# Hybrid decoder layer: other queue places for a SiLU, a reciprocal with its scaling, and the sums of the modulation

## The chip, the cores and the metric

The kernel runs on one core of a Trainium2 chip. The metric is the time of one execution on the device, in microseconds (us). The median of three executions before the change is 1846.04 us (1845.93 to 1848.33).

Five engines work side by side, each through a queue of its own: TensorE (PE in the profile, its weight loads PEld), VectorE (DVE), ScalarE (ACT), GpSimd (POOL) and SyncE (SP). In this kernel SP and POOL mostly issue DMA transfers. An instruction that waits holds up everything behind it in the same queue.

## The reference, cut to what matters

One layer of a hybrid decoder, 1024 tokens by 1024 channels, float32. Two branches start from the same projection: windowed attention with sinks, and a gated delta rule with 8 heads of 128 channels. Their gated sum passes an output projection and a norm, and an MLP of 4096 channels follows. A conditioning vector `c` gives six rows of modulation (`c_act @ w_ada + b_ada`). The change touches the delta rule's output and four of those rows:

```python
o = _gated_delta_rule(q, k, v, beta, g)                # head by head: a scan over chunks of tokens
o = o * lax.rsqrt(jnp.mean(jnp.square(o), -1, keepdims=True) + RMS_EPS) * norm_w
o = o * jax.nn.silu(z.reshape(shp))
...
mod = c_act @ w_ada[l] + b_ada[l]                      # shift, scale, gate rows
```

## The kernel before, in words

All large products are matmuls with a 512-column moving operand; float32 operands are split into a high and a low part, so that a product takes three matmuls. The kernel counts these large matmuls in `count[0]`, and this count is its clock for planning. `at(p, f)` puts the work `f` at count `p`, and `after(n, f)` n matmuls from now. Before each large matmul the events that are due are written out. So TensorE, VectorE and ScalarE have one fixed program order, written by hand; SP and POOL are ordered by the tile framework, by dependence.

The change lies in the stage of the heads. There, 24 projection units (`units_h`, 48 large matmuls each, through the line L261) fill TensorE: the q and v of each head and the gate `gb`. Between them the scan of the 8 heads runs, head `h` from count `R = R0 + 120 h`. Each head has 8 chunks of 128 tokens, one per 15 matmuls, in three steps 5 matmuls apart:

- `hd_a` at 0: TensorE multiplies the state (L1221), and VectorE makes `rhs` (L1223).
- `hd_b` at 5: TensorE multiplies `rhs` by the solved triangle (L1231), and ScalarE scales the result to `vn` (L1233).
- `hd_c` at 10: TensorE uses `vn` for the next state (L1242, added up by VectorE in L1247 and L1250) and for the output (L1254, L1255). ScalarE squares the output for the norm (L1257), VectorE copies it to `o` (L1258).

So each chunk goes through ScalarE once while TensorE does five large matmuls, and L1242 stands behind `vn` in TensorE's order.

Around the scan, the work of the other heads is placed: convolutions of q and v (ScalarE L1011 and L1012, VectorE taps L1016, ScalarE SiLU L1026), transposes and squares of q (L1166, L1170), products of k and q (L1182), transposes of v with ScalarE copies (L1205, L1209), the triangle of the next head (`hd_x`, L1147, with `hd_z` of the head after it, L1137), and the split of the next weights (ScalarE L232, VectorE L236).

For three kinds of work a small planner chooses the count. `vec(lag, cost, f)` and `act(lag, cost, f)` ask `window` for the first place from now + lag on. Per cycle of 15 matmuls VectorE has two windows (2 to 11 and 12 to 16.5) and ScalarE has one (7 to 19.5, so into the next cycle). A request uses up 0.68 of its cost in matmuls; if it doesn't fit any more, it moves to the next window. `now` writes work at a given count and books its cost. Outside the heads' range (`R0` to `R0 + 960`) `window` returns the count that was asked for.

The four parts that the change touches:

- **z.** `hd_gate` (at R + 35) loads the head's z into the tile `sz`, which exists once; POOL issues the load (L1121). The tile comes free when the previous head's result, which is written into the same tile (`hd_out`, L1287, at R + 45 and R + 60 of this head), has been stored (L1290). `hd_silu` applies SiLU to both halves on ScalarE (L1125).
- **The norm.** `hd_norm` (2 matmuls after the last chunk, so at 2 of the next head) adds two vectors on VectorE (L1263, L1264) and asks for `root`. `root` takes the square root on ScalarE (L1273), then come the reciprocal on VectorE (L1274), and the scaling of `o`, the even chunks on VectorE (L1270), the odd ones on ScalarE (L1268).
- **The output.** `hd_out` transposes `o` (L1284) and multiplies it with SiLU(z) (L1287).
- **The modulation.** Every 13 matmuls `ada_load` sends 256 KB of `w_ada` through SP (L1050) into one of three buffers, and VectorE adds it up (`ada_add`, L1058 and L1060). After eight of them `ada_part` sums over the partitions on TensorE (L1069).

When the last head is done (R0 + 960), the last `gb` unit runs, interleaved over its halves, and then the first unit of the next stage, the product with `w_oa`. In between ScalarE and VectorE split the attention's output into `ah` and `al` (`attn_split`, L218 and L219), and ScalarE empties the two PSUM banks of the `gb` unit (L1298). A unit takes two banks of the three of its kind.

Of the kernel before, what the change touches and what calls it, by code (L numbers as in the profile page):

```python
# [21 lines left out]
NT = S // P  # L22
# [12 lines left out]
def hybrid_layer_kernel(ctx: ExitStack, tc: tile.TileContext,  # L35
                        x, c, w_ada, b_ada, w_in, conv_w, a_log, dt_bias, sinks, dn_norm_w,
                        w_oa, w_ob, w_out, ln1_g, ln1_b, w_ff1, b_ff1, w_ff2, b_ff2,
                        ln2_g, ln2_b, out, dbg=None):
    nc = tc.nc
    x, c, out = x[0], c[0], out[0]  # L40
# [6 lines left out]
    V, A, G, T = nc.vector, nc.scalar, nc.gpsimd, nc.tensor  # L47
# [152 lines left out]
    def at(p, f, *args):  # L200
        order[0] += 1
        heapq.heappush(events, (p, order[0], f, args))

    def after(n, f, *args):
        at(count[0] + n, f, *args)
# [113 lines left out]
    def ada_load(blk):  # L319
        for i in range(2):  # L320
            t = ada_tile([P, 2, 4, P])
            for sec in (0, 1):
                nc.sync.dma_start(out=t[:, sec, :, :], in_=w_ada2[:, sec, 4 * i:4 * i + 4, blk * P:(blk + 1) * P])
            adav.setdefault(blk, []).extend(t[:, :, k, :] for k in range(4))
# [43 lines left out]
    for step in 'a0 x a1 x d a2 x a3 x a4 x a5 x a6 x a7 x'.split():  # L368
        if step == "x":
            x_load()  # L370
        elif step == "d":
            dk_raw = [load_raw(*wseq.pop(0)) for _ in range(2)]
            wdk = [parts_of(*r) for r in dk_raw]
        else:
            ada_load(int(step[1:]))
# [84 lines left out]
    for step in steps.split():  # L460
        f, k = step[0], int(step[1])
# [49 lines left out]
    with tc.tile_pool(name="pa", bufs=2, side="right") as pa:  # L511
# [120 lines left out]
        for h in range(8):  # L632
# [7 lines left out]
            for half in range(2):  # L640
                tp = psum("c", 1) if half else psum("b", 2)
                for j in range(4):
                    n = 4 * half + j
                    T.transpose(tp[:, j * P:(j + 1) * P], kT[:, n * P:(n + 1) * P], ident)
                for j in range(4):
                    n = 4 * half + j
# [16 lines left out]
            for half in range(2):  # L663
                kk = psum("a", 2)
                for j in range(4):
                    n = 4 * half + j
                    kc = kT[:, n * P:(n + 1) * P]
                    T.matmul(kk[:, j * P:(j + 1) * P], lhsT=kc, rhs=kc, start=True, stop=True)
                for j in range(4):
                    n = 4 * half + j  # L670
# [291 lines left out]
    def window(kind, p, cost):  # L962
        if not R0 <= p < R0 + 8 * PER:
            return p
        c, cost = int(p - R0) // 15 - 1, 0.68 * cost
        while True:
            for i, (start, cap) in enumerate({"V": ((2, 9), (12, 4.5)), "A": ((7, 12.5),)}[kind]):
                w = R0 + 15 * c + start
                q = max(p, w + used.get((kind, c, i), 0))
                if q + min(cost, cap) <= w + cap:  # L970
                    used[kind, c, i] = q + cost - w
                    return q
            c += 1
# [3 lines left out]
    def vec(lag, cost, f, *args):  # L977
        q = window("V", count[0] + lag, cost)
        at(q, f, *args)
        return q  # L980
# [9 lines left out]
    def act(lag, cost, f, *args):  # L990
        q = window("A", count[0] + lag, cost)
        at(q, f, *args)
        return q

    flags, padded = set(), []
# [49 lines left out]
    def ada_cols_of(f):  # L1045
        return (2, 5, 3, 4)[f // 2] * D + (f % 2) * HALF

    def ada_load(i, f, k):
        w, lo = ada["w"][i % 3], ada_cols_of(f)
        nc.sync.dma_start(out=w, in_=w_ada[k * P:(k + 1) * P, lo:lo + HALF])  # L1050
        q = vec(28, 3.3, ada_add, w, k)
        if k == KT - 1:
            at(q + 7, ada_part, f)

# [30 lines left out]
    for i, (f, k) in enumerate(items):  # L1085
        at(Q0 + 170 + 13 * i, ada_load, i, f, k)
# [40 lines left out]
    def o_chunk(d, n):  # L1127
        return d["o"][n // 4][:, chunk(n % 4)]
# [131 lines left out]
    def hd_norm(h):  # L1260
        d = heads[h]
        fs = pc.tile([P, NT], F32, tag="fs", name="fs")
        V.tensor_scalar(out=fs, in0=d["ssq"], scalar1=RMS_EPS * P * P, scalar2=None, op0=ALU.mult)  # L1263
        V.tensor_tensor(out=fs, in0=fs, in1=d["sso"], op=ALU.add)  # L1264

        def sc(n):
            if n % 2:
                A.activation(out=o_chunk(d, n), in_=o_chunk(d, n), func=AF.Copy, scale=fs[:, n:n + 1])  # L1268
            else:
                V.tensor_scalar(out=o_chunk(d, n), in0=o_chunk(d, n), scalar1=fs[:, n:n + 1], scalar2=None,  # L1270
                                op0=ALU.mult)
        def root():
            A.activation(out=fs, in_=fs, func=AF.Sqrt, scale=1.0 / P, bias=eps_q)  # L1273
            after(4, lambda: V.reciprocal(out=fs, in_=fs))  # L1274
            vec(5, 5.5, lambda: [sc(n) for n in range(0, NT, 2)])
            act(5, 7, lambda: [sc(n) for n in range(1, NT, 2)] + [flags.add(("o", h))])
        act(3, 7, root)

    def hd_out(h, half):
# [22 lines left out]
    for h in range(8):  # L1302
        R = R0 + PER * h
        early = max(R - 118, OPEN + 1)
        at(early, hd_load, h)
        for half in range(2):
            at(R - 45 + 15 * half, hd_kq, h, half)
            at(R - 40 + 15 * half, hd_qturn, h, half)
            at(R - 10 + 15 * half, hd_vturn, h, half)
            at(R + 75 + 5 * half, hd_silu, h, half)  # L1310
        if h == 0:
            at(early + 50, hd_z, 0)
            at(early + 52, hd_solved, 1)
        at(R - 55 if h else R0 - 30, hd_x, h)
        at(R + 35, hd_gate, h)
        for n in range(NT):
            at(R + 3 * HOP * n, hd_a, h, n)
            at(R + 3 * HOP * n + HOP, hd_b, h, n)
            at(R + 3 * HOP * n + 2 * HOP, hd_c, h, n)
        at(R + PER + 2, hd_norm, h)  # L1320
        at(R + PER + 45, hd_out, h, 0)
        at(R + PER + 60, hd_out, h, 1)
# [304 lines left out]
    for s in range(4):  # L1627
        q, t0 = (0, 1, 1, 0)[s], 4 * (s // 2)
# [324 lines left out]
    for s in range(7 * NS):  # L1953
        p = G0 + 24 * s
        at((p15 + 16, p15 + 28, p15 + 62, p15 + 64)[s] if s < 4 else p - 96 - 28, s_load, s)
        for j in range(2):
            if s < 2:
                q = p15 + (52, 68)[s] + 8 * j
            elif s >= 6 * NS:
                q = p - (94 if s > 6 * NS else 70) + (6 if s == 7 * NS - 1 else 10) * j  # L1960
            else:
                q = p - 46 + 10 * j
# [18 lines left out]
    for i, m in seq:  # L1981
        w, k0, mv, ab, begin = PROD[m]
# [152 lines left out]
```

## Time and profile before

| | |
|---|---|
| median of three executions | 1846.04 us |
| profiled execution | 1845.55 us, span 1843.8 us |
| TensorE busy | 1806.9 us (98%), mean granted clock 0.991 |
| VectorE, ScalarE, GpSimd busy | 1256.9, 1021.6, 309.8 us |
| heads' stretch, 560 to 960 us | TensorE busy 379.83 of 400 us, clock 0.97 |
| stretch before it, 192 to 560 us | TensorE busy 367.35 of 368 us, clock 1.00 |

A busy engine is one that has an instruction under way; the granted clock says at which share of its speed TensorE ran meanwhile. So a loss of TensorE can show up twice: as idle time, and as busy time at a lower clock. In a timeline, each row has the start, the duration, the engine, the line of the code, the operation, the tiles (`out<-in`) with shapes, the number of instructions that were merged, and in square brackets the idle time of the engine before it and what ended it. In a table of waits, a row says who waited for whom, the total, the number of times and the longest.

### The profile page before, as it was taken

The numbers are of one execution on the slowest core, as the hardware profiler recorded it, in microseconds if no ns is written. First come the engines' busy times: TensorE is split into PE (matmuls) and PEld (weight loads), VectorE is DVE, ScalarE is ACT, GpSimd is POOL, SyncE is SP. The second block draws the span as 40 slices with busy tenths as digits, with TensorE's granted clock in tenths as the row PEclk, the third lists the DMA queues.
The fourth block names the chain that finished last, engine by engine and source line by source line (L and its number), as shares of the span: only waits on it lengthen the run. The fifth ranks groups of instructions, "written<-read, shape, count | busy, mean of one in ns | idle before, by whom it ended". The sixth has DMA issues, their size and how long they took to land.

```text
span 1843.8 us, 26325 instructions
## 1 busy us (share of the span) xinstructions
PE 1806.9 (98%) x9185; PEld 1517.6 (82%) x9185; DVE 1256.9 (68%) x2366; ACT 1021.6 (55%) x2320; POOL 309.8 (17%) x466
## 2 busy tenths in 40 slices
PE   8999999999999999999889999999999999999998
PEld 6988888888888887888778888888888888888887
DVE  7688588888845565667344345788777776576697
ACT  4699678888765554555354223456555555434441
POOL 0233234443340011100001000001122220000000
PEclk8999999999999999999999999999999999999999
DMA  9666722232264556565447444358888879855671
GB/s 280 199 204 200 223 76 90 72 99 72 81 246 136 169 157 168 162 184 167 146 157 245 152 145 160 115 171 282 293 296 282 269 271 391 280 187 178 194 267 46
DMA packets 265686, 346.12 MB, mean 188 GB/s; under 512 B 26593, under 2 KB 171698, under 8 KB 265298
## 3 DMA queue, kind: packets, MB, share of 16 engines
q1 hardware_dynamic: 225938, 220.27, 38.2%
q0 software_dynamic: 31472, 107.39, 17.2%
q10 hardware_dynamic: 8144, 16.78, 2.5%
q8 instruction: 72, 1.18, 0.3%
q14 instruction: 60, 0.49, 0.1%
HBM read 235.59 MB, written 106.70 MB: 186 GB/s over the span
## 4 chain that ended last, share of the span: by engine, by line
PE 46%; issue 3%; ACT 2%; DVE 1%; DMA 0%; ACTq 0%; POOL 0%; DVEq 0%; POOLq 0%
PE mm L261 10%; PE mm L1996 8%; PE mm L2056 7%; PE a L2056 4%; PE b L1996 4%; PE b L2056 4%; PE a L1996 3%; PE mm L1622 2%; PE c L2056 2%; PE a L1622 1%; PE c L1622 1%; PE c L1996 0%; ACT mh L218 0%; ACT wh L218 0%; DMA sz<-z_d 0%
## 5 line engine op out<-in xcount | busy, mean ns | idle before, releaser
L261 PE MATMUL mm<-uh,wh 128*128 128x512 f32 x800 | 321.7, 402 | 0.0
L261 PE MATMUL mm<-uh,wl 128*128 128x512 f32 x800 | 321.6, 402 | 0.0
L261 PE MATMUL mm<-ul,wh 128*128 128x512 f32 x800 | 320.1, 400 | 0.0
L219 DVE TENSOR_TENSOR sp<-sraw,sp 128x1024 fp32r<-128x1024 f32 x112 | 132.7, 1219 | 75.9 <-ACT sp L218 75.9
L218 ACT ACTIVATE sp<-sraw 128x1024 fp32r<-128x1024 f32 x112 | 112.6, 1053 | 121.4 <-PE b L2056 75.4
L261 PEld LDWEIGHTS mm<-uh,wh 128*128 128x128 f32 x800 | 151.9, 190 | 26.6
L261 PEld LDWEIGHTS mm<-uh,wl 128*128 128x128 f32 x800 | 151.9, 190 | 26.2
L261 PEld LDWEIGHTS mm<-ul,wh 128*128 128x128 f32 x800 | 151.6, 189 | 26.3
L2056 PE MATMUL mm<-sp 128*128 128x512 f32 x528 | 136.0, 390 | 0.0
L2056 PEld LDWEIGHTS mm<-sp 128*128 128x128 f32 x528 | 98.7, 188 | 20.5 <-DVE sp L219 0.3
L2056 PE MATMUL a<-sp 128*128 128x512 f32 x336 | 92.2, 389 | 0.0
L824 DVE CUSTOM_DVE_ANT_0 nscore<-a,amask,nsink 128x256 f32<-128x256 f32 (+1 forms) x128 | 54.5, 463 | 43.7 <-PE a L817 43.4
L236 DVE TENSOR_TENSOR wl<-wr,wh 128x1024 fp32r<-128x1024 f32 x66 | 81.1, 1229 | 2.3 <-ACT wh L232 2.2
L1233 ACT ACTIVATE vn<-a,brk 128x128 f32<-128x128 f32 x64 | 23.4, 366 | 103.3 <-PE a L1231 103.1
L2056 PE MATMUL b<-sp 128*128 128x512 f32 (+1 forms) x336 | 79.6, 374 | 0.0
L2056 PEld LDWEIGHTS a<-sp 128*128 128x128 f32 x336 | 63.1, 188 | 13.1
L2056 PEld LDWEIGHTS b<-sp 128*128 128x128 f32 x336 | 60.3, 188 | 11.2
L232 ACT ACTIVATE wh<-wr 128x1024 fp32r<-128x1024 f32 x66 | 69.4, 1051 | 0.1
L835 POOL TENSOR_TENSOR sm<-sm 128x256 f32<-128x256 f32 x56 | 51.5, 920 | 103.8 <-ACT sm L831 73.0
L219 DVE TENSOR_TENSOR wl<-fraw,wh 128x1024 fp32r<-128x1024 f32 x43 | 52.5, 1221 | 19.6 <-ACT wh L218 19.6
L831 ACT ACTIVATE sm<-nscore,stat 128x257 f32<-128x257 f32 (+1 forms) x128 | 62.0, 487 | 2.7 <-DVE stat L824 2.5
L218 ACT ACTIVATE wh<-fraw 128x1024 fp32r<-128x1024 f32 x43 | 45.0, 1055 | 31.0 <-PE b L1996 24.8
(542 smaller groups left out, 4693.6 us busy)
## 6 DMA issues: line engine op xcount, KB each, us to landing
wr<-in_w_in_dram SPq DMA_DIRECT2D x60, 512.0 KB, 3.7
sraw<-hf_d SPq DMA_DIRECT2D x54, 512.0 KB, 4.4
adaw<-in_w_ada_dram SPq DMA_DIRECT2D x74, 256.0 KB, 5.0
fraw<-in_w_ff_dram SPq DMA_DIRECT2D x32, 512.0 KB, 5.4
sraw<-wt_d SPq DMA_DIRECT2D x32, 512.0 KB, 4.4
hf_d<-t ACTq DMA_DIRECT2D x48, 256.0 KB, 4.5
wt_d<-wx POOLq DMA_DIRECT2D x48, 256.0 KB, 3.6
sraw<-in_w_ff_dram SPq DMA_DIRECT2D x22, 512.0 KB, 4.9
```

Source lines behind the costliest of these rows:

```text
L218: A.activation(out=hi, in_=src, func=AF.Copy)
L219: after(lag, lambda: V.tensor_tensor(out=lo, in0=src, in1=hi.bitcast(F32), op=ALU.subtract))
L232: A.activation(out=hl[0], in_=raw, func=AF.Copy)
L236: V.tensor_tensor(out=hl[1], in0=raw, in1=hl[0].bitcast(F32), op=ALU.subtract)
L261: T.matmul(ts[half], lhsT=w[:, k, :], rhs=xx[k][:, sl], start=k == 0 and m == 0, stop=k == KT - 1 and m == 2)
L824: V.tensor_tensor_reduce(out=ns[:, i, 1:1 + W], in0=sc[:, i * 2 * P:i * 2 * P + W], in1=amask[:, mo:mo + W], scale=-1.0, scalar=nsink[:, 2 ...
L831: A.activation(out=sm[:, i, 0:1 + W], in_=ns[:, i, 0:1 + W], func=AF.Exp, scale=-1.0, bias=st[:, i:i + 1], accum_out=st[:, 2 + i:3 + i])
L835: G.tensor_tensor(out=sm[:, :, 1 + P:1 + 2 * P], in0=sm[:, :, 1:1 + P], in1=sm[:, :, 1 + P:1 + 2 * P], op=ALU.add)
L1233: after(1, lambda: A.activation(out=vn, in_=Wp[:, 0:P], func=AF.Copy, scale=brk[:, n, h:h + 1]))
L1622: T.matmul(pt, lhsT=m[k][:, tok], rhs=w[:, k % 2, :], start=k == 0 and w is wh and m is mh, stop=k == KT - 1 and m is ml)
L1996: T.matmul(pt, lhsT=a[:, kk, :], rhs=b[k], start=begin and k == 0 and x_ == 0, stop=k == 3 and x_ == 2, skip_group_check=True)
L2056: T.matmul(to, lhsT=a[:, f, t * P:(t + 1) * P], rhs=b[:, f, lo:up], start=(begin or own) and s % NS == 0 and f == 0 and x_ == 0, stop=s % ...
```

## The change

Three edits, in the counts and helpers that place work; the instructions themselves stay the same.

1. `hd_silu` moves from R + 75 and R + 80 to R + 122 and R + 130, which is 2 and 10 matmuls into the next head's scan.
2. In `root`, the reciprocal goes from a fixed 4 matmuls later to VectorE's planner, 9 matmuls later, at a cost of 0.5; both halves of the scaling are asked for 11 instead of 5 matmuls later.
3. `ada_add` is asked for 33 instead of 28 matmuls after its load was written.

```diff
     def ada_load(i, f, k):
         w, lo = ada["w"][i % 3], ada_cols_of(f)
         nc.sync.dma_start(out=w, in_=w_ada[k * P:(k + 1) * P, lo:lo + HALF])
-        q = vec(28, 3.3, ada_add, w, k)
+        q = vec(33, 3.3, ada_add, w, k)
         if k == KT - 1:
             at(q + 7, ada_part, f)
...
             A.activation(out=fs, in_=fs, func=AF.Sqrt, scale=1.0 / P, bias=eps_q)
-            after(4, lambda: V.reciprocal(out=fs, in_=fs))
-            vec(5, 5.5, lambda: [sc(n) for n in range(0, NT, 2)])
-            act(5, 7, lambda: [sc(n) for n in range(1, NT, 2)] + [flags.add(("o", h))])
+            vec(9, 0.5, lambda: V.reciprocal(out=fs, in_=fs))
+            vec(11, 5.5, lambda: [sc(n) for n in range(0, NT, 2)])
+            act(11, 7, lambda: [sc(n) for n in range(1, NT, 2)] + [flags.add(("o", h))])
...
             at(R - 10 + 15 * half, hd_vturn, h, half)
-            at(R + 75 + 5 * half, hd_silu, h, half)
+            at(R + 122 + 8 * half, hd_silu, h, half)
```

## The prediction

> **What bounds the kernel now.** I read the page first, then busy time by stretch, then the waits of the heads' stretch, and then the timeline around the longest of them.
>
> ```profile
> span 1843.8 us, 26325 instructions
> ...
> PE 1806.9 (98%) x9185; PEld 1517.6 (82%) x9185; DVE 1256.9 (68%) x2366; ACT 1021.6 (55%) x2320; POOL 309.8 (17%) x466
> ```
>
> ```profile
> 192.00:560.00 368.00, 367.35 (x1936) 314.41 (x1935) 283.39 (x688) 278.65 (x848) 145.83 (x185) 1.00 0.38 121
> 560.00:960.00 400.00, 379.83 (x2302) 324.57 (x2301) 236.06 (x549) 210.86 (x619) 32.29 (x53) 0.97 0.53 156
> ```
>
> TensorE is busy for 98% of the span, so only its gaps and its clock leave something to gain. The second view (length, busy time of PE, PEld, DVE, ACT and POOL, granted clock, DMA share) puts both losses into the heads' stretch: 400 − 379.83 = 20.2 us idle, at a mean clock of 0.97. The stretch before has neither. The waits of the heads' stretch (total, times, longest) name the cause:
>
> ```profile
> ACT vn L1233 <- PE a L1231: 103.1, 53, 4.5
> ...
> ACT sz L1125 <- DMA sz<-z_d: 32.8, 6, 8.5
> ...
> POOL sz L1121 <- DMA og_d<-sz: 23.1, 7, 6.4
> ...
> PE a L1242 <- ACT vn L1233: 17.7, 6, 5.1
> ...
> DVE fs L1274 <- ACT fs L1273: 16.2, 8, 3.6
> ...
> ACT L1125 <- DMA sz<-z_d: 5.3, 1, 5.3
> ...
> PE a L1231 <- DVE rhs L1223: 2.3, 4, 1.3
> ```
>
> TensorE waits 17.7 us for `vn`, in six places, and 2.3 us for `rhs`. That is nearly all of the 20.2. ScalarE mostly waits for TensorE (103.1 us), which is harmless; but in 6 + 1 places its queue stands at the SiLU of z until z has landed, 38.1 us in all, since the load waits until the result of the head before has left the tile. Head 1, ScalarE and then TensorE:
>
> ```profile
> 635.32 0.37 ACT L1233 ACTIVATE vn<-a,brk 128x128 f32<-128x128 f32 x1 [2.84 <-PE a L1231]
> ...
> 640.34 0.37 ACT L1233 ACTIVATE vn<-a,brk 128x128 f32<-128x128 f32 x1 [0.82 <-PE a L1231]
> ...
> 649.86 0.63 ACT L1125 ACTIVATE sz<-sz 128x512 f32<-128x512 f32 x1 [6.05 <-DMA sz<-z_d]
> 650.39 0.35 ACT L1233 ACTIVATE vn<-a,brk 128x128 f32<-128x128 f32 x1
> ```
>
> ```profile
> 650.80 0.49 PE L1242 MATMUL a<-vn,kd 128*128 128x128 f32 x2 [2.20 <-ACT vn L1233]
> ...
> 652.45 0.63 PE L261 MATMUL mm<-uh,wl 128*128 128x512 f32 x1
> ```
>
> The SiLU stands 6.05 us for its data with the next `vn` behind it, and TensorE idles 2.20 us. Two microseconds later its matmuls take 0.63 us each. The clock tells why; these are 4.5 us behind each of the six stalls of TensorE, in order of time:
>
> ```profile
> 651.00:655.50 4.50, 4.50 (x22) 4.12 (x22) 2.62 (x5) 3.02 (x13) 0.00 (x0) 0.62 0.18 58
> 700.00:704.50 4.50, 4.50 (x20) 3.94 (x20) 1.55 (x5) 0.98 (x8) 0.00 (x0) 0.64 0.32 101
> 744.60:749.10 4.50, 4.50 (x32) 4.18 (x33) 2.58 (x8) 3.19 (x13) 0.35 (x1) 1.00 0.05 16
> 835.10:839.60 4.50, 4.50 (x30) 4.06 (x31) 3.21 (x10) 3.16 (x13) 0.00 (x0) 1.00 0.20 60
> 883.20:887.70 4.50, 4.50 (x17) 4.02 (x18) 1.28 (x3) 1.85 (x11) 0.00 (x0) 0.52 0.35 117
> 930.10:934.60 4.50, 4.50 (x15) 3.92 (x16) 0.66 (x3) 1.72 (x4) 0.00 (x0) 0.50 0.16 58
> ```
>
> Behind four of them the clock falls to 0.62, 0.64, 0.52 and 0.50. Behind the other two it stays at 1.00. The lost share is 4.5 × (0.38 + 0.36 + 0.48 + 0.50) = 7.7 us.
>
> **The change part by part: the SiLU.** Moved from 75 to 122 matmuls, it comes long after its data: in head 1 the data is there at 649.86, and a chunk of 15 matmuls lasts 5.0 us (635.32 to 640.34), so 34 to 47 matmuls later is 11 to 15 us later. The load and the store are not moved; POOL's order depends on the tile, not on the SiLU. The reader of SiLU(z) (`hd_out`, 45 and 60 into the next head) stays 35 and 30 matmuls behind it, some 10 us. So the stalls go, and with them their clock losses: **−17.7 − 7.7 = −25.4 us**. The idle time alone, if the clock fell for another reason, is the lower end: −17.7.
>
> What the SiLU meets at its new place is a fuller ScalarE queue: root, second half of v's copies, convolutions, scaling. The first half (2 into the next head) fits into the idle time before the first `vn`, which is part of the 103.1 us. The second half (10) asks for a place in the window from 7 to 19.5. There the root has booked 0.68 × 7 = 4.76 and v's copies 0.68 × 5.5 = 3.74, to 15.5. With a convolution's SiLU (1.84) already there it still fits, before the second `vn` (21). Where a weight split (3.2) is booked too, 11.7 of 12.5 are gone, and it goes behind the second `vn`. Head 2 is of this second kind, head 5 of the first:
>
> ```profile
> 669.21 1.09 ACT L232 ACTIVATE wh<-wr 128x1024 fp32r<-128x1024 f32 x1
> ...
> 671.94 0.20 DVE L1274 RECIPROCAL fs<-fs 128x8 f32<-128x8 f32 x1 [1.00 <-ACT fs L1273]
> 672.06 0.30 DVE L1223 SCALAR_TENSOR_TENSOR rhs<-a,negegc,vr 128x128 f32<-128x128 f32 x1
> 672.41 0.49 PE L1231 MATMUL a<-rhs,TT 128*128 128x128 f32 x2 [0.35 <-DVE rhs L1223]
> ...
> 673.00 0.37 ACT L1233 ACTIVATE vn<-a,brk 128x128 f32<-128x128 f32 x1 [0.84 <-PE a L1231]
> ...
> 673.89 0.38 PE L1242 MATMUL a<-vn,kd 128*128 128x128 f32 x2
> ```
>
> ```profile
> 808.24 1.28 ACT L1026 ACT_TABLE_LOAD   x1
> ...
> 809.53 0.63 ACT L1026 ACTIVATE qT<-qT 128x512 f32<-128x512 f32 x1
> 810.07 0.35 ACT L1233 ACTIVATE vn<-a,brk 128x128 f32<-128x128 f32 x1
> ...
> 810.48 0.49 PE L1242 MATMUL a<-vn,kd 128*128 128x128 f32 x2
> ```
>
> In head 2, L1242 comes 0.89 us after `vn` starts; where it truly waits (head 1 above) 0.41 us. So a `vn` may be 0.48 us late for nothing. In head 5 that slack is used up, and a further SiLU costs its full 0.53 us (649.86 to 650.39). In heads 1 and 3 I take 0.1 each, an estimate between 0 and that 0.53. Head 7 has no convolution SiLU left to share the table load with:
>
> ```profile
> 904.26 0.37 ACT L1233 ACTIVATE vn<-a,brk 128x128 f32<-128x128 f32 x1 [0.67 <-PE a L1231]
> ```
>
> This is its second `vn`, ahead of which ScalarE idles 0.67 us: 1.28 + 0.53 − 0.48 − 0.67 = 0.7 us. Together **+1.4 us**. The ends are 0 and 7 × (1.28 + 0.53 − 0.48) = 9.3 us.
>
> **The end of the last head** has no planner any more: the last SiLU stands at R0 + 962 and R0 + 970, with the square root (965) between them and the emptying of the PSUM banks (993) behind. ScalarE works there without a gap:
>
> ```profile
> 945.19 1.28 ACT L1273 ACT_TABLE_LOAD   x1
> ...
> 950.90 1.05 ACT L1298 ACTIVATE gz<-mm 128x512 f32<-128x512 f32 x2
> ```
>
> ```profile
> 951.52 0.50 PE L261 MATMUL mm<-ah,wh 128*128 128x512 f32 x1
> ```
>
> The matmul at 951.52 is the first into the bank that L1298 empties; it already comes right behind it. The first SiLU adds 0.53, and the second adds a new table load and 0.53, since the root has put its own table in: 2.34 us on ScalarE, and on TensorE. A stall of 2.34 is nearest to that of 2.20, after which the clock cost 4.5 × 0.38 = 1.7. So **+4.0 us**; the ends are 0 (if ScalarE has drawn ahead) and 4.0.
>
> [...]
>
> **Reciprocal and scaling.** In head 2 the reciprocal stands in VectorE's queue before `rhs` and waits for the root; TensorE loses 0.35 us. The 2.3 us of waits for `rhs` are four: three of this kind, and one of 1.3. At 9 after the root, about 19 into the head, the reciprocal comes behind that `rhs` (16), and the root is done by then: **−1.0 us**. The ends are 0 and −1.0. The scaling stays some ten matmuls ahead of its reader (45), so it costs nothing; without this cover the transposes of L1284 would wait for the shift, 6 matmuls or 2 us.
>
> **The sums of the modulation.** The fourth wait for `rhs` (1.3 us) lies behind a sum whose data was late:
>
> ```profile
> 769.01 0.76 DVE L1060 SCALAR_TENSOR_TENSOR ada<-ada,c_col 128x512 f32<-128x512 f32 x1 [2.06 <-DMA ada<-in_w_ada_dram]
> ```
>
> Five matmuls are 1.7 us, most of the 2.06. But a sum frees the buffer for a later load, so loads move too, with the weight loads behind them in SP's queue; those are issued a unit or more ahead. I take half, **−0.6 us**, with 0 and −1.3 as ends.
>
> **The sum:** −25.4 + 1.4 + 4.0 − 1.0 − 0.6 = −21.6 us. The profiled execution took 1845.55 us with a span of 1843.8, and the median is 0.5 us above it. So the profiled time comes to 1823.9, a median to 1824.4; I say 1824.
>
> **Rivals.** *Better:* ScalarE catches up at the last head's end and no `vn` is late: −25.4 − 1.0 − 1.3 = −27.7, 1818. For it speaks that the planner moves other work out of the window; against it that ScalarE shows no gap at that end.
>
> *The stall moves to the head's start:* the second SiLU with its table load stands before the second `vn` in all seven heads, 9.3 instead of 1.4 us: −13.7, 1832. For it speaks head 5, with no slack left; against it head 2, where it doesn't fit there.
>
> *Slower:* the SiLU takes the planner's place of a convolution, which moves on by a cycle of 15 matmuls (5 us). Then the transposes and products of the next head wait. In head 1 the cover is 5.7 us:
>
> ```profile
> 638.89 0.63 ACT L1026 ACTIVATE qT<-qT 128x512 f32<-128x512 f32 x1
> ```
>
> ```profile
> 644.57 1.06 PE L1182 MATMUL b<-qT,kT 128*128 128x128 f32 x8
> ```
>
> From a delay above that on, TensorE waits for the rest: a tap (of the size of the sum above, 0.76), a table load and a SiLU (1.28 + 0.63), and the clock after it, 1.7: 4.4 us. Once per head that is 31 us: −21.6 + 31 = +9, 1855. Against it: two moves would have to meet to use the cover up.
>
> *The SiLU still waits:* z would have to land over 11 us later than in head 1. The longest wait here was 8.5 us. Then 1846.
>
> **How the numbers follow.** The forecast has 0.74, better 0.08, the stall moved 0.12, slower 0.03, still waiting 0.03. The range leaves out the last two and the edges of the rest: 1817 to 1833. Less than 0.2% (3.7 us) a measurement of this kernel can hardly tell from no change: faster 0.94, same 0.03, slower 0.03.
>
> **What would show it.** The rows L1125 <- DMA and PE a L1242 <- ACT vn nearly vanish, and the clock in the heads' stretch reaches 1.00 but for the end. Around the first matmuls of the next stage TensorE waits over 2 us for L1298. L1274 no longer waits for L1273. Wrong it would be if waits for `vn` gather at the second chunk of each head, or L1182, L1166 or L1205 begin to wait for a convolution.

## The result, and the profile after

The changed kernel takes 1823.56 us (median of four, 1822.89 to 1823.72), the kernel before on the same chip 1845.99 us. The ratio is 0.988, with an interval of 0.986 to 0.990. The profiled execution took 1822.89 us with a span of 1821.2. Page of the changed kernel, then its heads' stretch in the view of busy time by stretch:

```profile
span 1821.2 us, 26309 instructions
...
PE 1798.4 (99%) x9184; PEld 1513.4 (83%) x9185; DVE 1258.2 (69%) x2366; ACT 1022.7 (56%) x2321; POOL 310.6 (17%) x466
```

```profile
560.00:960.00 400.00, 395.06 (x2409) 338.90 (x2408) 249.02 (x566) 223.65 (x638) 34.64 (x57) 1.00 0.59 175
```

TensorE now idles 4.9 of 400 us there instead of 20.2, and its mean clock is 1.00 instead of 0.97. The waits of that stretch; the second fence holds TensorE's alone, in the stretch from 540 to 1000 us:

```profile
ACT vn L1233 <- PE a L1231: 103.6, 52, 3.7
...
POOL sz L1121 <- DMA og_d<-sz: 21.0, 7, 4.9
...
DVE ada L1060 <- DMA ada<-in_w_ada_dram: 2.4, 1, 2.4
```

```profile
PE mm L261 <- ACT gz L1298: 2.4, 1, 2.4
PE a L1242 <- ACT vn L1233: 1.1, 2, 0.6
PE c L1254 <- DVE o L1258: 1.0, 1, 1.0
PE a L1231 <- DVE rhs L1223: 0.4, 2, 0.2
```

The row in which L1125 waits for its DMA is gone from the list. The load of z itself is as late as before: POOL still waits for the store of the result ahead of it, 21.0 us in seven places (before 23.1). But no instruction of ScalarE stands in the queue for it any more. Of TensorE's 17.7 us of waits for `vn`, 1.1 are left. L1274 no longer waits for L1273 except once for 0.3 us. What is new is the wait of 2.4 us for L1298 at the end of the last head, and one of 1.0 us at L1254 for VectorE's copy L1258, which stands behind a late sum.

For the comparisons below I use a length that leaves out the program's first part: from the start of the first `vn` to the first matmul into the bank that L1298 empties, read off the timeline. I call it the length of the heads.

| kernel | first `vn` at | that matmul at | length of the heads | rest of the span |
|---|---|---|---|---|
| before | 579.54 | 951.52 | 371.98 us | 892.28 us |
| changed | 580.65 | 928.39 | 347.74 us | 892.81 us |

The heads give 24.2 us, and 1.6 us come back outside of them: the first `vn` is 1.1 us later, and the rest is 0.5 us longer. No edit touches either part. In other executions the first `vn` starts anywhere from 579.2 to 584.3 us. One execution, of the kernel with only the SiLU at 104 and 112 below, took 2565.31 us at a granted clock of 0.654; the medians and ratios leave it out.

### The profile page after: what moved, and what is told of

It is laid out like the page before. It is cut to its first block, busy times and chain, and to the rows that moved or that the text cites. A ratio compares the mean times of both kernels' runs of the same rounds, so it can differ in the third digit from the quotient of the medians.

```text
span 1821.2 us, 26309 instructions
## 1 busy us (share of the span) xinstructions
PE 1798.4 (99%) x9184; PEld 1513.4 (83%) x9185; DVE 1258.2 (69%) x2366; ACT 1022.7 (56%) x2321; POOL 310.6 (17%) x466
## 3 DMA queue, kind: packets, MB, share of 16 engines
q0 software_dynamic: 31472, 107.39, 17.7%
## 4 chain that ended last, share of the span: by engine, by line
PE 86%; DVE 4%; ACT 3%; DMA 3%; issue 1%; POOL 0%; ACTq 0%; DVEq 0%; POOLq 0%; SPq 0%
PE mm L261 39%; PE mm L1996 7%; PE mm L2056 6%; PE a L2056 4%; PE b L2056 4%; PE b L1996 4%; PE a L1996 2%; PE c L2056 2%; PE c L891 2%; PE mm L1622 1%; PE mm L191 1%; PE mm L189 1%; PE mm L190 1%; DMA ada<-in_w_ada_dram 1%; PE a L817 1%
```

## The experiments

**The SiLU alone, and the two other edits alone.** Three kernels, each with one edit of the change:

```diff
-            at(R + 75 + 5 * half, hd_silu, h, half)
+            at(R + 122 + 8 * half, hd_silu, h, half)
```

> The SiLU of z alone at its new places, reciprocal, scaling and sums as before. Theory (the SiLU carries the gain): no wait of L1125 for its DMA, TensorE's waits for vn fall from 17.7 to about 1 us, the wait for rhs stays at about 2.3 us, a wait of about 2.4 us for L1298 at the end of the last head; 1824 to 1826 us. Rival (the reciprocal and the sums carry a share): over 1830 us.

Measured: 1823.87 us, ratio 0.988 (0.986 to 0.990), the same as the whole change. Heads 348.22 us. TensorE's waits:

```profile
PE a L1231 <- DVE rhs L1223: 2.6, 4, 1.5
PE mm L261 <- ACT gz L1298: 2.4, 1, 2.4
PE a L1242 <- ACT vn L1233: 0.6, 1, 0.6
```

The theory holds: the SiLU carries the gain, the waits for `rhs` stay, and the wait for L1298 comes with it.

```diff
-            after(4, lambda: V.reciprocal(out=fs, in_=fs))
-            vec(5, 5.5, ...)
-            act(5, 7, ...)
+            vec(9, 0.5, lambda: V.reciprocal(out=fs, in_=fs))
+            vec(11, 5.5, ...)
+            act(11, 7, ...)
```

> Reciprocal and scaling of the norm alone at their new places. Theory: L1274 no longer waits for L1273 (before 16.2 us), the waits of TensorE for rhs fall from 2.3 us in four places to one of about 1.3 us behind the late sum; those for vn stay at 17 to 18 us with their clock losses; about 1845 us. Rival (the waits for rhs have another cause): 2 us or more stay in four places.

In this kernel the planner puts the reciprocal of head 5 behind the scaling of its odd chunks, so these are scaled with the root and not with its reciprocal. The instructions and their number are the same, but the result is not the layer's: this kernel serves for its times alone. Measured: 1848.72 us in one execution, some 4 us above the expectation; heads 374.30 us. L1274 waits for L1273 once, for 0.3 us. TensorE's waits:

```profile
PE a L1242 <- ACT vn L1233: 20.7, 7, 5.9
PE a L1231 <- DVE rhs L1223: 2.1, 1, 2.1
```

The three short waits for `rhs` are gone, as expected. The one behind the late sum is left, here with 2.1 us. The waits for `vn` did not stay at 17 to 18 us: in head 4 the planner now puts the SiLU of z before a `vn` that stood ahead of it, and TensorE waits 2.02 us there. So the time says nothing of the gain of some 1 us.

```diff
-        q = vec(28, 3.3, ada_add, w, k)
+        q = vec(33, 3.3, ada_add, w, k)
```

> The sums of the modulation alone 5 matmuls later. Theory (the data of one sum was late by 2.06 us, and 5 matmuls are 1.7 us): VectorE waits 0.4 us or less for that transfer, and the wait for rhs of 1.3 us goes. Rival (the load moves later with the sum that frees its buffer): VectorE still waits 1.5 us or more, and TensorE for it. Waits for vn stay at 17 to 18 us; about 1845 us.

Measured: 1838.57 us, one execution, some 9 us below the kernel before (1847.95 on that chip, 1844.52 to 1850.12). That was in nobody's expectation. Heads 363.97 us, 8.0 less than before. TensorE's longest wait and, from the list of all waits, VectorE's for the data of the sum:

```profile
PE a L1242 <- ACT vn L1233: 13.2, 4, 4.7
```

```profile
DVE ada L1060 <- DMA ada<-in_w_ada_dram: 0.7, 1, 0.7
```

The late sum did get its data in time here, as the theory said. But the 8 us come from somewhere else: there are four stalls for `vn` instead of six. In heads 2 and 6 the planner now puts the SiLU of z behind the next `vn`. In head 5 its place is the same, but it waits 2.85 us for z instead of 5.42, and the stall is gone. In head 4 it goes the other way: the SiLU moves before a `vn`, and a stall of 2.74 us is new. Head 2 on ScalarE:

```profile
698.33 0.63 ACT L1125 ACTIVATE sz<-sz 128x512 f32<-128x512 f32 x1 [1.56 <-DMA sz<-z_d]
...
702.05 0.37 ACT L1233 ACTIVATE vn<-a,brk 128x128 f32<-128x128 f32 x1 [1.28 <-PE a L1231]
```

The SiLU still waits 1.56 us for z, but the `vn` after it still finds ScalarE idle and waiting for TensorE. Sums five matmuls later shift VectorE's windows and with them the convolutions, and a convolution's SiLU (L1026) takes the place in ScalarE's window: in head 2 the one that started at 689.72 us before starts at 693.08. In the whole change this effect has nothing left to save.

**The late data without a move.** Does the stall come from z alone, or is the old place bad by itself? The old places, with a second tile for z, so that its load need not wait for the store:

```diff
-        heads[h]["sz"] = big4("sz", bufs=1)
+        heads[h]["sz"] = big4("sz", bufs=2)
...
-            t = big4("gz", shape=[P, HALF])
+            t = big4("vr")[:, 0:HALF] if i == 7 and half else big4("gz", shape=[P, HALF], bufs=1)
```

> The kernel before with two tiles for z instead of one, so that z can be loaded a head earlier; all places as before. To make room the copies of the gb units use one tile instead of two (the very last one borrows another tile). Theory (the stall is the late data and nothing else): L1125 no longer waits for its DMA, the waits for vn fall under 1 us, the clock in the heads' stretch rises to 1.00, the 25.4 us go without any cost at the heads' starts and ends, the waits for rhs stay; about 1821 us. Rival (the old place is bad by itself, among the squares of q and the copies): waits for vn of 5 us or more stay, over 1830 us.

Measured: 1821.62 us, ratio 0.987 (0.985 to 0.988). Heads 347.45 us. TensorE waits in one line only:

```profile
PE a L1231 <- DVE rhs L1223: 3.1, 4, 2.0
```

No wait for `vn` is left at the old place, and every SiLU of z stands behind the same `vn` as before. This is the term of the SiLU by itself: 371.98 − 347.45 = 24.5 us. Against it stand 0.8 us by which the waits for `rhs` grew, and the clock behind the longest of these: it is at 0.50 from 763.0 to 766.4 us, which costs 1.7 us.

**How far must the SiLU go?** The kernel before, with the SiLU asked for 6 matmuls later:

```diff
-            at(R + 75 + 5 * half, hd_silu, h, half)
+            at(R + 81 + 5 * half, hd_silu, h, half)
```

> The kernel before with only the SiLU moved, by 6 matmuls (to 81 and 86), which the planner turns into a place behind the next vn, one chunk or 5 us later than before. Theory (only the lateness of z counts, and the stalls of 0.9 to 5.1 us were what was left of it after the slack of one vn): some waits of L1125 for its DMA stay, but those for vn fall from 17.7 to at most 2 us, with no wait for L1298; 1821 to 1824 us. Rival (the gain needs the place at the head's end): waits for vn of 8 us or more, over 1833 us.

Measured: 1822.60 us, ratio 0.986 (0.984 to 0.988), heads 349.37 us. TensorE's waits:

```profile
PE a L1231 <- DVE rhs L1223: 2.5, 4, 1.4
PE a L1242 <- ACT vn L1233: 2.3, 1, 2.3
```

The 2.3 us are slightly more than expected and lie in the last head, where the SiLU also loads its table. ScalarE there:

```profile
911.28 1.28 ACT L1125 ACT_TABLE_LOAD   x1 [3.44 <-DMA sz<-z_d]
912.58 1.15 ACT L1125 ACTIVATE sz<-sz 128x512 f32<-128x512 f32 x2
...
913.88 0.36 ACT L1233 ACTIVATE vn<-a,brk 128x128 f32<-128x128 f32 x1
```

The SiLU stands one `vn` later than before in heads 2, 6 and 7, two later in heads 1, 3 and 5, and where it was in head 4, where no stall had been. So one or two chunks of delay remove five of the six stalls; the place at the end of the head is not needed.

**The end of the last head.** In the changed kernel ScalarE's chain there ends as follows, and then TensorE goes on:

```profile
923.72 1.28 ACT L1125 ACT_TABLE_LOAD   x1
...
925.01 0.63 ACT L1125 ACTIVATE sz<-sz 128x512 f32<-128x512 f32 x1
...
927.76 1.05 ACT L1298 ACTIVATE gz<-mm 128x512 f32<-128x512 f32 x2
```

```profile
928.39 0.50 PE L261 MATMUL mm<-ah,wh 128*128 128x512 f32 x1 [2.42 <-ACT gz L1298]
```

Two kernels take this apart: one with the last head's second SiLU right behind the first, before the square root, so that no table is loaded between; the other with both of them earlier.

```diff
-            at(R + 122 + 8 * half, hd_silu, h, half)
+            at(R + 122 + (1 if h == 7 else 8) * half, hd_silu, h, half)
```

> The changed kernel with the last head's second SiLU put right behind the first, before the square root, so that no table is loaded between them. Theory (the wait for L1298 is the sum of a table load of 1.28 us and two SiLUs of 0.53): the wait falls from 2.4 to 1.1 us, and the clock behind it stays at 1.00. Rival (it hangs on something else): 2.4 us stay.

Measured: 1820.83 us in one execution; the wait is

```profile
PE mm L261 <- ACT gz L1298: 1.0, 1, 1.0
```

The clock stays at 1.00 behind it.

```diff
-            at(R + 122 + 8 * half, hd_silu, h, half)
+            at(R + 122 + 8 * half if h < 7 else R + 95 + 5 * half, hd_silu, h, half)
```

> The changed kernel, but the last head's SiLU at 95 and 100 matmuls into its own head, after its data and before the square root. Theory (the 2.4 us wait for L1298 at the end of the last head are the two SiLUs and the extra table load ahead of it on ScalarE, 2.34 us): that wait falls to 0.1 us or less, and the time to about 1821 us. Rival (ScalarE is late there because of the splits of the attention's output): the wait stays over 2 us, the time at 1823 to 1824 us.

Measured: 1819.97 us, ratio 0.986 (0.984 to 0.988), heads 343.93 us. No wait of a matmul for L1298 is left. From 2.42 to 1.0 to nothing: by these differences the table load (1.28 us in its row) is 1.4 of it and the two SiLUs 1.0. The heads became shorter by 3.8 us and not by 2.4. Of the 1.4 us between, 1.0 is the wait at L1254: the late sum waited only 0.6 us for its data in this execution, and that wait was not there.

**A version that is better than the change.** The SiLU behind the landing of z, but before the crowded start of the next head:

```diff
-            at(R + 122 + 8 * half, hd_silu, h, half)
+            at(R + 104 + 8 * half, hd_silu, h, half)
```

> The changed kernel with the SiLU at 104 and 112 matmuls into its own head instead of 122 and 130. Theory (any place after the landing of z does): the two waits for vn at the second chunk (0.5 us each) and that for L1298 (2.4 us) go, no new ones come; about 1820 us. Rival (the place after the head's end matters, since ScalarE is crowded before it): new waits for vn of 3 us or more, 1824 us or more.

Measured: 1819.55 us, ratio 0.986 (0.983 to 0.988), heads 343.75 us. Of TensorE's waits 0.6 us for `rhs` and 0.4 for `vn` are left, the latter at a new place in head 4, behind a convolution's SiLU with its table load of 1.28 us. Once more beside the changed kernel on one chip:

> The changed kernel once more, beside the two that follow. Theory (its last stall of 2.4 us costs a clock loss of 1.7 us in some executions and none in others): 1823 to 1825 us, the wait for L1298 at 2.4 us again, the clock behind it 1.00 or about 0.7.

> The changed kernel with the SiLU at 104 and 112 matmuls into its own head, once more beside the changed kernel on the same chip. Theory: 2.4 us less for L1298, 0.7 us less for vn, and now and then the clock loss: 3 to 5 us below the changed kernel, 1819 to 1820 us. Rival (those stalls were hidden by something later): within 1.5 us of it.

Measured: the changed kernel 1824.81 us (1821.94 to 1825.12), this one 1818.31 us (1817.29 to 1820.13), ratio to the kernel before 0.984 (0.983 to 0.986). That is 6.5 us between them, more than the 5 expected. In the heads it is 347.32 − 343.65 = 3.7 us, which is within the forecast. Another 4.1 us of the two profiled executions lie ahead of the first `vn` (583.31 against 579.20), which no edit touches. There TensorE stands 1.58 us before L816 in the slower one, from 220.5 us on, and the clock is 0.52 from 223.5 to 227.0 us, another 1.7; the other execution has neither. So 3.3 of the 4.1 us are not the edit's. Busy time of the heads' stretch for the one at 104:

```profile
560.00:960.00 400.00, 398.90 (x2427) 342.20 (x2426) 251.55 (x570) 222.53 (x637) 36.14 (x60) 1.00 0.61 180
```

TensorE idles 1.1 of 400 us. What the two smaller edits add there, the kernel before with only the SiLU at 104 and 112 should show:

> The kernel before with only the SiLU moved, to 104 and 112 matmuls. Against the run above it shows what the other two edits add there. Theory (only the waits for rhs, 2.3 us in four places, and 0.15 us at each): 1 to 3 us above that run, 1821 to 1822 us, waits for rhs of 2 to 3 us. Rival (the other two edits shift the planner's places to a disadvantage): at or below that run.

> The same kernel as the last one of the run before (only the SiLU moved, to 104 and 112), for an undisturbed profile. Where are the 4 to 6 us that it takes above the run with all three edits? Theory (waits for rhs in four places, the longest behind the late sum): waits for rhs of 2.5 to 4 us, TensorE idle 2 to 4 us more over the heads than the 1.1 us there. Rival (a stall that lowers the clock, at vn or at L1298): a wait of over 2 us at one of those and a clock under 0.8 behind it. Third (nothing in the heads; a matter of the program's first 60 us): the heads take at most 2 us longer than there.

Measured: ratio 0.987 both times (0.985 to 0.989, and 0.984 to 0.990), 1824.08 us in the first, on the same chip as the run with all three edits, and 1822.82 us in the second, on another chip. That is 5.8 and 4.5 us above that run, more than the 1 to 3 expected. Heads 348.08 us in the second, 4.4 us longer, and TensorE idles 4.0 of 400 us instead of 1.1. Its waits:

```profile
PE a L1231 <- DVE rhs L1223: 2.5, 2, 2.2
PE a L1242 <- ACT vn L1233: 1.4, 1, 1.4
```

Neither waits for z. The first is the reciprocal and the late sum. The second lies in head 6, where a table load (1.28 us) and a convolution's SiLU (0.63 us) stand before a `vn`; behind it the clock is at 0.50 from 852.6 to 856.0 us, which costs 1.7 us. So the 4.4 us are 2.9 us of idle time and 1.7 us of clock, within 0.2: in this execution the other two edits earn more than I priced, because one of these stalls reached the clock.

## Why the prediction was right, point by point

**What bounds the kernel** was read rightly: the SiLU's wait, one queue further TensorE's wait, and the clock behind it. The kernel with two tiles shows it as directly as can be: no SiLU moves, the data comes earlier, and 24.5 us go. That is 0.9 short of the −25.4 forecast for the SiLU, but part of the closeness is luck: with the 0.8 us of `rhs` and the 1.7 us of clock that came in there, the term is some 27.0 (an estimate from these rows), 1.6 more than forecast.

**The clock as a term of its own** was needed. Idle time alone would have given −17.7, and the kernel with two tiles measures 24.5. The term was a little too small: it looked at 4.5 us behind each stall, while behind the last one the clock stays at 0.50 until 935.33 us. Where the clock is at 0.50, TensorE is busy for 3.41, 3.40, 4.37 and 5.29 us, and half of this is 8.2 us instead of 7.7. About 1 us of the 27.0 stays open.

**The new place** cost what was forecast. The second SiLU goes before the second `vn` in head 5, and TensorE waits 0.56 us there (forecast 0.53); this is ScalarE and then TensorE:

```profile
799.86 0.61 ACT L1125 ACTIVATE sz<-sz 128x512 f32<-128x512 f32 x1
800.38 0.35 ACT L1233 ACTIVATE vn<-a,brk 128x128 f32<-128x128 f32 x1
...
800.78 0.49 PE L1242 MATMUL a<-vn,kd 128*128 128x128 f32 x2 [0.56 <-ACT vn L1233]
```

Head 7 waits 0.5 (forecast 0.7), heads 1 and 3 nothing (0.1 each).

**The end of the last head** had the right mechanism and the right wait, 2.42 for 2.34 us. The clock loss that I added from the nearest row, 1.7 us, did not come in the profiled execution; it did come in the kernel with the SiLU alone. The step that failed is "a stall of 2.34 is nearest to that of 2.20": the term measured +2.4 and not +4.0.

**The reciprocal**: the three waits for `rhs` behind it are gone, in the edit alone too, and the mechanism of the −1.0 stands. In the changed kernel two waits of 0.21 us are new at the same step of two heads, behind a convolution's tap (L1016) on VectorE, so 0.6 to 0.7 us are left of it.

**The sums**: this pair of profiles gives some −0.3 instead of −0.6. The wait for the data did not shrink (2.06 us before, 2.37 after), and TensorE loses 1.0 us for it in L1254 and not 1.3 in L1231. Over all the executions the step looks better: with the sums asked for 28 matmuls after their load VectorE's longest wait for such data is 2.1 to 3.0 us and TensorE's behind it 1.3 to 2.2, with 33 it is 0.6 to 2.4 and 0 to 1.0. Whether the loads moved with the sums, as the counterargument said, is not shown. What the edit does alone, to move the SiLU of z in three heads through the planner, was not seen at all.

**The sum**: from the first to the last `vn` the changed kernel needs 334.71 us and the one before 361.32, so −26.6; the terms that lie there gave −25.4 + 1.4 − 1.0 − 0.6 = −25.6. By the estimates above, a SiLU term that was too small and gains of the smaller edits that were too large offset each other in this. The end cost 1.6 less than forecast, and the parts outside the heads 1.6 us more, where nothing was forecast. These two cancel, and part of the closeness of 1824 to 1823.56 is that luck.

**The rivals**: in no kernel did L1182, L1166 or L1205 begin to wait for a moved convolution. L1166 waited once, for 1.0 us with the sums alone, and that was for the squares (L1170). The stall did not move to the heads' starts. The time of the better case, 1818, is what the version at 104 reaches, but by another place of the SiLU and not by a ScalarE that catches up.

## What to carry to other kernels

Where an engine's queue stands at a transfer, ask what is queued behind it, and how late that may come: here 6 us of waiting were 2 us of TensorE's time, and one or two chunks of delay for the waiting instruction were nearly enough. Count the clock behind a stall as part of its price, but as a chance and not as a fixed sum: behind a wait of 2.4 us for L1298 it was 1.7 us in one trace and nothing in two. And where work is placed by a planner with windows, an edit on one engine can move work on another; so look at the new order, and don't add up the gains of single edits.

## What the runs showed of the hardware that I had not expected

A stall of the same length at the same place lowers the clock in one execution and not in another. The wait for L1298 was 2.42 us in the changed kernel and 2.40 us with the SiLU alone. The stretch behind it, first of the changed kernel:

```profile
930.00:934.50 4.50, 4.50 (x24) 3.69 (x23) 4.50 (x8) 2.89 (x5) 1.06 (x2) 1.00 0.68 194
```

The same with the SiLU alone:

```profile
932.00:934.50 2.50, 1.96 (x7) 1.58 (x8) 1.78 (x4) 2.50 (x7) 0.00 (x0) 0.84 0.93 312
934.50:939.00 4.50, 4.50 (x17) 3.66 (x17) 3.43 (x7) 2.54 (x5) 1.06 (x2) 0.71 0.60 171
```

In the first the clock stays at 1.00; in the second the loss is 2.5 × 0.16 + 4.5 × 0.29 = 1.7 us. The repetition of the changed kernel had 2.41 us of wait and a clock of 1.00. Before the change, 2.20 us did lower it, and 0.91 and 1.58 us did not.

The traces show where the first two differ. In the kernel before, the clock is at 0.50 for 3.41 us from 652.02 and from 699.81 us, and for 6.83 us from 880.72 and from 928.50 us. These starts lie 47.79, 180.91 and 47.78 us apart, which is 14, 53 and 14 times 3.413, so in this trace the clock changes at fixed steps. These are such steps around the stall at L1298, counted on from the other changes of the clock in the same trace (in the changed kernel it rises from 0.50 to 1.00 at 22.64 us, 264 such steps before 923.77). First the SiLU alone, then the changed kernel:

```profile
926.88:930.30 3.42, 3.26 (x15) 2.36 (x13) 2.57 (x4) 3.42 (x7) 0.00 (x0) 1.00 0.48 159
930.30:933.71 3.41, 1.17 (x5) 1.00 (x6) 1.48 (x3) 3.40 (x8) 0.00 (x0) 1.00 0.62 192
933.71:937.12 3.41, 3.41 (x12) 2.71 (x11) 2.34 (x5) 3.33 (x6) 1.06 (x2) 0.50 0.53 150
```

```profile
923.77:927.18 3.41, 2.19 (x10) 1.50 (x8) 3.41 (x10) 3.40 (x7) 0.00 (x0) 1.00 0.25 93
927.18:930.59 3.41, 2.20 (x10) 1.81 (x11) 1.74 (x4) 3.41 (x9) 0.00 (x0) 1.00 0.89 292
930.59:934.01 3.42, 3.42 (x19) 2.82 (x17) 3.42 (x7) 2.30 (x4) 1.06 (x2) 1.00 0.53 154
```

With the SiLU alone 2.24 us of the stall lie in one step, and the next one has a clock of 0.50. In the changed kernel 1.22 us lie in one step and 1.21 in the next, in its repetition 1.77 and 0.64, and the clock stays. So in these three traces the clock goes with the place of the stall among the steps; no run shifted that place alone. A fixed bound does not come out of these runs: 1.35 us in one step were followed by 0.50 in the kernel with only the SiLU at 104 and 112, and 1.58 us in one step were not in the kernel before.
